# Moving the transposes of the forget gates behind the latent keys, and the scan's row of ones to GpSimd

## The chip, the cores and the metric

The kernel runs on one core of one Trainium2 chip. The core has TensorE (matrix products and transposes, into eight PSUM banks), VectorE, ScalarE, GpSimd, a queue for loads (SP), and DMA engines. The metric is the device time of one execution in microseconds, lower is better; it is given as the median of several runs.

## What is computed

The program is a decoder trunk of two layers over 512 positions of width 1024, in float32. The change lies in the first layer's mixer, of which this is the part that matters:

```python
h = x @ w_in
q_a, c_kv, q_idx, k_idx, w_idx, q_b, k_b, v_b, f_in = _split(h, EVEN_WIDTHS)
q_idx = q_idx.reshape(bsz, seq, H_IDX, D_IDX) * (D_IDX ** -0.5)
w_idx = w_idx * (H_IDX ** -0.5)
log_f = jax.nn.log_sigmoid(f_in + b_f)
cum_f = jnp.cumsum(log_f, axis=1)
...
idx = jnp.einsum('bthd,bsd->bths', qi, k_idx)
score = jnp.einsum('bth,bths->bts', wi, jax.nn.relu(idx))
...
_, sel = lax.top_k(score, k_sel)
...
lb = jnp.einsum('bthd,bshd->bhts', qb, k_b)
lb = lb + jnp.swapaxes(fq, 1, 2)[..., None] - cum_f_keys[:, :, None, :]
```

Eight heads attend over keys chosen by an index score (128 of up to 512), eight others over all earlier keys with a bias made of cumulated logarithms of forget gates. After the mixer come a norm, a convolutional feed-forward part, and the second layer.

## The kernel before

**Products.** All weights come as units of 128 x 1024 float32 through one stream on the SP queue (three raw buffers). Each unit is split into a high part (a cast on ScalarE, line 76) and a low part (a subtraction on VectorE, line 77), and each product is made of three, high by high, high by low and low by high (lines 168 to 170, in `mm3`). A projection (`proj`, line 183) is eight blocks of three products into one PSUM bank. `unit()` hands out the next split unit and has the two after it split too; the units for the values and the first pairs go to larger buffers (lines 387 and 388), and the others share three.

**The first stage** (lines 359 to 410). Two units are computed side by side, one of which gives, for all positions, the index keys in rows 0 to 63, the forget gates in rows 64 to 71 and the index weights in rows 96 to 103. That bank is copied to a temporary buffer `cw` (line 370). On the eight rows of the gates follow the bias (378), the steps of a logarithm of a sigmoid (379 to 382), a row of ones (383, VectorE) and a scan over the positions (384, VectorE) that writes the cumulated gates back into `cw`; they are stored to DRAM (386, GpSimd's queue), from where they are later loaded as biases along the keys. Meanwhile TensorE computes the other three index query projections, whose banks are scaled and split by ScalarE (399) and VectorE (400) in turn.

**Around the change.** Then TensorE transposes `cw` (403 to 405), and ScalarE scales two slices of the result: `nfq` (408), the cumulated gates along the queries, read by GpSimd's bias (line 550), and `wi` (410), the index weights, read by VectorE's accumulation of the scores (453, 455). Behind that stand the projection of the latent keys (413, 414), and the relative-position table: two small products with a one-hot table (422, 428), their copies (424, 430), two round trips through DRAM on GpSimd's queue (426 to 435) and a mask (436). Then the scores: for each of three blocks of positions and eight heads two products (448) into a bank of their own, a rectifier on ScalarE (450) and an accumulation on VectorE (453, 455). Behind them stand the value projections (484 to 489), the attention loop (678 on) with the rounds of the selection on VectorE (467, 469, 472) spread over it, and the rest of the program.

**What sets the order.** The text gives dependencies and priorities; a planner (`schedule_with_timeline_sim=True`) lays out each engine's queue from a timeline of its own and may put a later instruction ahead of an earlier one. On the chip each engine runs its queue in order. Temporary buffers come from a pool of eight, banks from a pool of eight. The selection's rounds are tied to a named VectorE instruction ahead of each (line 468).

Of the kernel before, what the change touches and what calls it, by code (L numbers as in the profile page):

```python
# [9 lines left out]
F32 = mybir.dt.float32  # L10
FR = mybir.dt.float32r
AF = mybir.ActivationFunctionType
ALU = mybir.AluOpType
# [5 lines left out]
NCH = 4  # L19
HD = 64  # L20
NH = 8
# [13 lines left out]
def _f(ap):  # L35
    return ap.bitcast(F32)
# [55 lines left out]
def _body(ctx, tc, A):  # L92
    nc = tc.nc
# [10 lines left out]
    def bank():  # L104
        return ps.tile([128, 512], F32, name="bank")

    def temp():
        return tmp.tile([128, 512], F32, name="temp")
# [7 lines left out]
    def unit():  # L116
        i = base[0]
        base[0] += 1
        return ws.get(i)
# [35 lines left out]
    ident = cst.tile([128, 128], F32)  # L155
# [27 lines left out]
    def proj(w, xt):  # L183
        p = bank()
        half(w, xt, p, 0, S)
        return p
# [8 lines left out]
    def proj_t(us, xt, n):  # L195

        p = bank()
        for k in range(8):
            o = (k % 2) * 512
            last_mm[0] = mm3(p, xk(xt, k, n * 128, n * 128 + 128), wk(us[k // 2], o, o + 512), k == 0, k == 7)  # L200
        return p
# [148 lines left out]
    with ExitStack() as m0:  # L350
        M = m0.enter_context
        mc = M(tc.tile_pool(name="mc", bufs=1))
# [10 lines left out]
        for k in range(8):  # L363
            for u in range(FIRST):
                a = 128 if u else 0
                w = w0[u][1:]
                mm3(p0[u][:, a:], wk(w, k * 128, k * 128 + 128), xk(xq, k, a), k == 0, k == 7)
        p = p0[0]
        cw = temp()
# [4 lines left out]
        nc.vector.tensor_copy(misc[64:128, 1], _f(misc[0:64, 1]))  # L374
        z = temp()
        e = temp()
        g = slice(64, 72)
        nc.scalar.activation(z[g], cw[g], AF.Identity, bias=bf[g])
        nc.vector.scalar_tensor_tensor(out=e[g], in0=z[g], scalar=-1.0, in1=z[g], op0=ALU.mult, op1=ALU.max)
        nc.scalar.activation(e[g], e[g], AF.Exp, scale=-1.0)  # L380
        nc.scalar.activation(e[g], e[g], AF.Ln, bias=1.0)
        nc.vector.scalar_tensor_tensor(out=z[g], in0=z[g], scalar=0.0, in1=e[g], op0=ALU.min, op1=ALU.subtract)
        nc.vector.memset(e[g], 1.0)
        nc.vector.tensor_tensor_scan(out=cw[g], data0=e[g], data1=z[g], initial=0.0, op0=ALU.mult, op1=ALU.add)
        fk_d = dr.tile([NH, S], F32, name="fk_d")
        nc.gpsimd.dma_start(fk_d, cw[g])
        for k in range(6, 10):
# [4 lines left out]
        for m in range(4):  # L392
            if m < FIRST - 1:
                p = p0[1 + m]
            else:
                p = bank()
                half(unit(), xq, p, 128, S)
            for s, (a, b) in enumerate(((slice(0, 64), slice(64, 128)), (slice(64, 128), slice(0, 64)))):
                nc.scalar.mul(qi[s][a, m, late_q], p[a, late_q], float(HD ** -0.5))
                nc.vector.scalar_tensor_tensor(out=qi[s][b, m, late_q], in0=p[a, late_q], scalar=float(HD ** -0.5),  # L400
                                               in1=_f(qi[s][a, m, late_q]), op0=ALU.mult, op1=ALU.subtract)

        p = bank()
        for n in range(NCH):
            nc.tensor.transpose(p[:, n * 128:n * 128 + 128], cw[:, n * 128:n * 128 + 128], ident)
        p3 = p.rearrange("p (a b) -> p a b", a=4)
        nfq = mc.tile([128, NCH, NH], F32)
        nc.scalar.mul(nfq, p3[:, :, 64:72], -1.0)
        wi = mc.tile([128, NCH, NH], F32)
        nc.scalar.mul(wi, p3[:, :, 96:104], float(NH ** -0.5))  # L410


        p = proj(unit(), xq)
# [7 lines left out]
        p = bank()  # L421
# [5 lines left out]
        p = bank()  # L427
# [7 lines left out]
                                      ap=[[383, 128], [128 * 384, NH], [1, 256]]))  # L435
        nc.gpsimd.affine_select(out=T5[:, :, 128:], in_=T5[:, :, 128:], pattern=[[0, NH], [-1, 128]],
                                compare_op=ALU.is_ge, fill=BIG, base=0, channel_multiplier=1)


        sel = [None] + [mc.tile([128, 128 * (j + 1)], F32, name=f"sel{j}") for j in (1, 2, 3)]  # L440
# [45 lines left out]
        for n in range(NCH):  # L486
            p = proj_t(us, xq, n)
# [224 lines left out]
    with ExitStack() as m1:  # L712
        M = m1.enter_context
        mc = M(tc.tile_pool(name="mc1", bufs=1))
# [15 lines left out]
        for n in range(NCH):  # L730
            p = proj_t(us, xt, n)
# [12 lines left out]
            for gi in range(8):  # L744
                nc.vector.tensor_scalar(t[:, gi], t[:, gi], mv[:, gi, 0:1], ve[:, gi:gi + 1],
                                        op0=ALU.subtract, op1=ALU.mult)
# [6 lines left out]
        for n in range(NCH):  # L753
            p = proj_t(us, xt, n)
# [3 lines left out]
        for gp in range(4):  # L758
            p = bank()
# [5 lines left out]
            for j in range(2):  # L765
# [3 lines left out]
                    out=uq[:, :, f], in0=p[:, j * 256:j * 256 + 256].rearrange("p (a b) -> p a b", a=4),  # L769
                    scalar=sb[:, gi:gi + 1], in1=uq[:, :, f], op0=ALU.add, op1=ALU.mult)  # L770
        oq = [quad() for _ in range(4)]
        for ft in range(4):
            p = bank()
# [111 lines left out]
```

## Time and profile before

| | us |
|---|---|
| median of three runs | 1191.61 |
| lowest and highest of them | 1191.40, 1192.16 |
| the profiled execution | 1195.23 |
| its span, first to last instruction | 1193.5 |
| TensorE busy in the span | 1165.9 |
| VectorE, ScalarE, GpSimd busy | 720.0, 471.8, 152.1 |
| mean granted clock of TensorE | 0.988 |

The profile is one execution. "Busy" of TensorE is modelled, since products are pipelined: the start of the next product says more than the length of one. A row of a timeline gives the start, the length, the engine (PE is TensorE, DVE VectorE, ACT ScalarE, POOL GpSimd), the line of the kernel, what it writes and reads, and, in brackets, how long the engine was idle before it and what ended that. The granted clock is a share of the full 2.4 GHz; it has the levels 1.00 and 0.50, and a slice with a change in it shows a mean.

### The profile page before, as it was taken

The page shows a single profiled execution, that of the slowest core. Times are in us where ns is not written, and L with a number is a line of the kernel's source. Part 1 is how long each engine was busy: PE and PEld are TensorE (multiplying, and loading weights), DVE is VectorE, ACT ScalarE, POOL GpSimd, SP SyncE. Part 2 cuts the span into 40 slices and gives each one's busy share as a digit, 9 for nine tenths or more (in the row PEclk, how much of TensorE's full clock was granted, in tenths as well). Part 3 has the DMA queues.
Part 4 walks back from the last instruction along what each step waited for, and adds up shares of the span by engine and source line. Part 5 has one row for each costly group of instructions (what it writes and reads, how often), then busy time and mean ns, then how long its engine had stood idle before and what let it go on. Part 6 is the DMA issues. An engine that isn't in the chain of part 4 may idle for free. (4 is left out here: it accounts for less than half of the span.)

```text
span 1193.5 us, 14505 instructions
## 1 busy us (share of the span) xinstructions
PE 1165.9 (98%) x5519; PEld 968.4 (81%) x5519; DVE 720.0 (60%) x1219; ACT 471.8 (40%) x751; POOL 152.1 (13%) x238
## 2 busy tenths in 40 slices
PE   8899999989999999999999999999999999999997
PEld 7687877778988888888888788889888888888885
DVE  6789988847565666563236974456665656552226
ACT  6615667732334443442123343232444444432221
POOL 1033535303000000010001410003000000010003
PEclk9899999989999999999999999999999999999999
DMA  7434201132132323243334223372223232344221
GB/s 236 162 100 146 89 9 46 65 135 101 54 105 90 102 92 102 93 148 117 129 127 151 98 89 114 120 244 88 71 90 105 90 104 89 123 141 142 88 89 70
DMA packets 39973, 129.89 MB, mean 109 GB/s; under 512 B 5128, under 2 KB 5136, under 8 KB 39904
## 3 DMA queue, kind: packets, MB, share of 16 engines
q1 hardware_dynamic: 34848, 113.26, 29.0%
q0 software_dynamic: 5056, 15.71, 4.1%
q8 instruction: 43, 0.70, 0.2%
q14 instruction: 26, 0.21, 0.1%
HBM read 120.54 MB, written 9.99 MB: 109 GB/s over the span
## 5 line engine op out<-in xcount | busy, mean ns | idle before, releaser
L77 DVE TENSOR_TENSOR wlo<-raw,whi 128x1024 fp32r<-128x1024 f32 x159 | 194.9, 1227 | 291.6 <-ACT whi L76 290.8
L168 PE MATMUL bank<-quad,whi 128*128 128x512 f32 (+2 forms) x932 | 354.7, 382 | 2.6 <-ACT whi L133 1.9
L170 PE MATMUL bank<-quad,wlo 128*128 128x512 f32 (+2 forms) x932 | 354.8, 381 | 0.0
L169 PE MATMUL bank<-quad,whi 128*128 128x512 f32 (+2 forms) x932 | 354.3, 380 | 0.0
L76 ACT CAST whi<-raw 128x1024 fp32r<-128x1024 f32 x159 | 167.4, 1054 | 266.6 <-PE bank L170 119.6
L168 PEld LDWEIGHTS bank<-quad,whi 128*128 128x128 f32 x932 | 175.9, 189 | 36.7 <-ACT whi L133 2.2
L170 PEld LDWEIGHTS bank<-quad,wlo 128*128 128x128 f32 x932 | 176.1, 189 | 32.6
L169 PEld LDWEIGHTS bank<-quad,whi 128*128 128x128 f32 x932 | 176.0, 189 | 32.6
L169 PE MATMUL bank<-wlo,quad 128*128 128x512 f32 x388 | 151.9, 392 | 0.0
L170 PE MATMUL bank<-whi,quad 128*128 128x512 f32 x388 | 151.6, 392 | 0.0
L168 PE MATMUL bank<-whi,quad 128*128 128x512 f32 x388 | 150.4, 392 | 0.0
L168 PE MATMUL bank<-quad 128*128 128x512 f32 (+5 forms) x280 | 99.7, 360 | 0.5 <-ACT quad L206 0.5
L169 PE MATMUL bank<-quad 128*128 128x512 f32 (+5 forms) x280 | 98.6, 353 | 0.7 <-DVE quad L77 0.6
L170 PE MATMUL bank<-quad 128*128 128x512 f32 (+5 forms) x280 | 98.6, 353 | 0.0
L169 PEld LDWEIGHTS bank<-wlo,quad 128*128 128x128 f32 x388 | 73.5, 190 | 15.5
L168 PEld LDWEIGHTS bank<-whi,quad 128*128 128x128 f32 x388 | 73.5, 190 | 15.4
L170 PEld LDWEIGHTS bank<-whi,quad 128*128 128x128 f32 x388 | 73.4, 189 | 15.2
L225 POOL DMA_DIRECT2D temp<-x x24 | 13.2, 548 | 568.0 <-ACT quadx L336 424.6
L305 DVE SCALAR_TENSOR_TENSOR temp<-bank,fcw,temp 128x511 f32<-128x511 f32 x88 | 65.4, 743 | 9.1 <-ACT temp L304 9.1
L307 DVE SCALAR_TENSOR_TENSOR temp<-bank,fcw,temp 128x510 f32<-128x510 f32 x88 | 65.8, 748 | 3.0
L304 ACT ACTIVATE temp<-bank,fcw 128x512 f32<-128x512 f32 x88 | 59.9, 681 | 10.8 <-PE bank L170 10.8
L332 ACT ACTIVATE temp<-temp 128x512 f32<-128x512 f32 x44 | 27.8, 633 | 88.5 <-DVE temp L307 88.5
(148 smaller groups left out, 1280.2 us busy)
## 6 DMA issues: line engine op xcount, KB each, us to landing
raw<-in_ws_dram SPq DMA_DIRECT2D x190, 512.0 KB, 3.5
x<-temp SPq DMA_DIRECT2D x24, 256.0 KB, 2.0
temp<-x POOLq DMA_DIRECT2D x24, 256.0 KB, 3.2
temp<-in_xT_dram SPq DMA_DIRECT2D x8, 256.0 KB, 6.5
temp<-fk_d SPq DMA_DIRECT2D x8, 256.0 KB, 4.9
temp<-in_x_dram POOLq DMA_DIRECT2D x8, 256.0 KB, 3.1
quad<-in_ln_g_dram POOLq DMA_DIRECT2D x4, 512.0 KB, 5.3
quad<-in_ln_b_dram POOLq DMA_DIRECT2D x4, 512.0 KB, 6.0
```

The source lines that it names most:

```text
L76: nc.scalar.copy(hi, t)
L77: dve[0] = nc.vector.tensor_tensor(out=lo, in0=t, in1=_f(hi), op=ALU.subtract)
L168: nc.tensor.matmul(out, a[0], b[0], start=first, stop=False)
L169: nc.tensor.matmul(out, a[0], b[1], start=False, stop=False)
L170: return nc.tensor.matmul(out, a[1], b[0], start=False, stop=last)
L225: nc.gpsimd.dma_start(t, src[n * 128:n * 128 + 128, hf * 512:hf * 512 + 512])
L304: nc.scalar.mul(t, p, cw[:, j, 2:3])
L305: nc.vector.scalar_tensor_tensor(out=t[:, 1:], in0=p[:, :S - 1], scalar=cw[:, j, 1:2], in1=t[:, 1:], op0=ALU.mult, op1=ALU.add)
L307: nc.vector.scalar_tensor_tensor(out=t[:, 2:], in0=p[:, :S - 2], scalar=cw[:, j, 0:1], in1=t[:, 2:], op0=ALU.mult, op1=ALU.add)
L332: nc.scalar.activation(tg, tg, AF.Silu)
```

## The change

The memset of the row of ones (line 383) goes from VectorE, where it reused the buffer `e`, to GpSimd, with a temporary buffer of its own; the scan reads that buffer. The four transposes and the two scalings (403 to 410) are written behind the table's mask (436, 437), so behind the projection of the latent keys and the table products and ahead of the scores. What is computed stays the same.

```diff
--- before.py
+++ after.py
@@ -374,14 +374,15 @@
         nc.vector.tensor_copy(misc[64:128, 1], _f(misc[0:64, 1]))
         z = temp()
         e = temp()
+        one = temp()
         g = slice(64, 72)
         nc.scalar.activation(z[g], cw[g], AF.Identity, bias=bf[g])
         nc.vector.scalar_tensor_tensor(out=e[g], in0=z[g], scalar=-1.0, in1=z[g], op0=ALU.mult, op1=ALU.max)
         nc.scalar.activation(e[g], e[g], AF.Exp, scale=-1.0)
         nc.scalar.activation(e[g], e[g], AF.Ln, bias=1.0)
         nc.vector.scalar_tensor_tensor(out=z[g], in0=z[g], scalar=0.0, in1=e[g], op0=ALU.min, op1=ALU.subtract)
-        nc.vector.memset(e[g], 1.0)
-        nc.vector.tensor_tensor_scan(out=cw[g], data0=e[g], data1=z[g], initial=0.0, op0=ALU.mult, op1=ALU.add)
+        nc.gpsimd.memset(one[g], 1.0)
+        nc.vector.tensor_tensor_scan(out=cw[g], data0=one[g], data1=z[g], initial=0.0, op0=ALU.mult, op1=ALU.add)
         fk_d = dr.tile([NH, S], F32, name="fk_d")
         nc.gpsimd.dma_start(fk_d, cw[g])
         for k in range(6, 10):
@@ -399,15 +400,6 @@
                 nc.scalar.mul(qi[s][a, m, late_q], p[a, late_q], float(HD ** -0.5))
                 nc.vector.scalar_tensor_tensor(out=qi[s][b, m, late_q], in0=p[a, late_q], scalar=float(HD ** -0.5),
                                                in1=_f(qi[s][a, m, late_q]), op0=ALU.mult, op1=ALU.subtract)
-
-        p = bank()
-        for n in range(NCH):
-            nc.tensor.transpose(p[:, n * 128:n * 128 + 128], cw[:, n * 128:n * 128 + 128], ident)
-        p3 = p.rearrange("p (a b) -> p a b", a=4)
-        nfq = mc.tile([128, NCH, NH], F32)
-        nc.scalar.mul(nfq, p3[:, :, 64:72], -1.0)
-        wi = mc.tile([128, NCH, NH], F32)
-        nc.scalar.mul(wi, p3[:, :, 96:104], float(NH ** -0.5))
 
 
         p = proj(unit(), xq)
@@ -435,6 +427,15 @@
                                       ap=[[383, 128], [128 * 384, NH], [1, 256]]))
         nc.gpsimd.affine_select(out=T5[:, :, 128:], in_=T5[:, :, 128:], pattern=[[0, NH], [-1, 128]],
                                 compare_op=ALU.is_ge, fill=BIG, base=0, channel_multiplier=1)
+
+        p = bank()
+        for n in range(NCH):
+            nc.tensor.transpose(p[:, n * 128:n * 128 + 128], cw[:, n * 128:n * 128 + 128], ident)
+        p3 = p.rearrange("p (a b) -> p a b", a=4)
+        nfq = mc.tile([128, NCH, NH], F32)
+        nc.scalar.mul(nfq, p3[:, :, 64:72], -1.0)
+        wi = mc.tile([128, NCH, NH], F32)
+        nc.scalar.mul(wi, p3[:, :, 96:104], float(NH ** -0.5))
 
 
         sel = [None] + [mc.tile([128, 128 * (j + 1)], F32, name=f"sel{j}") for j in (1, 2, 3)]
```

## Rows read from the trace of the kernel before

**Rows 1.** Profile page, part 1, by engine: busy us (share), xinstructions.

```profile
PE 1165.9 (98%) x5519; PEld 968.4 (81%) x5519; DVE 720.0 (60%) x1219; ACT 471.8 (40%) x751; POOL 152.1 (13%) x238
```

**Rows 2.** Who waited for whom, TensorE, whole span: us in total, times, longest us.

```profile
PE bank L405 <- DVE temp L384: 5.9, 1, 5.9
```

**Rows 3.** Timeline of TensorE, 37 to 56 us: start, length, what, [idle before].

```profile
37.83 1.08 PE L405 MATMUL bank<-ident,temp 128*128 128x128 f32 x4 [5.88 <-DVE temp L384]
...
38.56 0.78 PE L168 MATMUL bank<-quad,whi 128*128 128x512 f32 x1
...
46.10 0.81 PE L422 MATMUL bank<-temp,rb 32*8 32x384 f32 x2
...
47.15 8.62 PE L448 MATMUL bank<-quad 128*128 128x256 f32 x48
```

**Rows 4.** Busy time in half microseconds, all engines; PEclk is the granted clock.

```profile
core 0: us, PE busy (x) PEld busy (x) DVE busy (x) ACT busy (x) POOL busy (x), PEclk, DMA share, GB/s
...
35.50:36.00 0.50, 0.00 (x0) 0.00 (x0) 0.47 (x2) 0.24 (x1) 0.00 (x0) 0.80 0.88 319
...
42.50:43.00 0.50, 0.50 (x3) 0.40 (x2) 0.00 (x0) 0.00 (x0) 0.00 (x0) 0.87 1.12 188
```

**Rows 5.** Timeline of ScalarE: the copy of the second chunk of value products.

```profile
66.69 0.59 ACT L206 CAST quad<-bank 128x512 fp32r<-128x512 f32 x1 [4.85 <-PE bank L170]
```

**Rows 6.** Timeline of VectorE, 34 to 48 us.

```profile
34.10 0.48 DVE L383 MEMSET temp<- 8x512 f32 x1 [0.16 <-DVE quad L77]
34.62 1.23 DVE L77 TENSOR_TENSOR quad<-raw,quad 128x1024 fp32r<-128x1024 f32 x1
...
36.47 1.22 DVE L384 TENSOR_TENSOR_SCAN temp<-temp 8x512 f32<-8x512 f32 x1
37.71 0.55 DVE L400 SCALAR_TENSOR_TENSOR quad<-bank,quad 64x384 fp32r<-64x384 f32 x1
...
40.69 0.56 DVE L400 SCALAR_TENSOR_TENSOR quad<-bank,quad 64x384 fp32r<-64x384 f32 x1
47.06 1.23 DVE L77 TENSOR_TENSOR wlo<-raw,whi 128x1024 fp32r<-128x1024 f32 x1 [5.81 <-ACT whi L76]
```

**Rows 7.** Timeline of GpSimd, the first 40 us.

```profile
0.79 0.20 POOL L156 MEMSET ident<- 128x128 f32 x1 [0.29 <-POOLq L874]
...
38.25 0.53 POOL L386 DMA_DIRECT2D fk_d<-temp  x1 [26.12 <-DVE temp L384]
```

**Rows 8.** Timeline of ScalarE, 33 to 50 us.

```profile
33.81 0.99 ACT L399 ACTIVATE quad<-bank 64x384 fp32r<-64x384 f32 x2
...
37.35 1.04 ACT L76 CAST whi<-raw 128x1024 fp32r<-128x1024 f32 x1 [1.61 <-DMA raw<-in_ws_dram]
38.42 0.48 ACT L399 ACTIVATE quad<-bank 64x384 fp32r<-64x384 f32 x1
...
39.04 0.19 ACT L410 ACTIVATE wi<-bank 128x32 f32<-128x32 f32 x1
45.98 1.04 ACT L76 CAST whi<-raw 128x1024 fp32r<-128x1024 f32 x1 [6.75 <-PE bank L169]
...
47.41 0.47 ACT L424 ACTIVATE temp<-bank 8x384 f32<-8x384 f32 x1
...
47.85 2.20 ACT L450 ACTIVATE temp<-bank 128x256 f32<-128x256 f32 x8
```

**Rows 9.** Timeline of TensorE behind a later pause.

```profile
224.92 0.44 PE L168 MATMUL bank<-pt,quad 128*64 128x512 f32 x1 [1.41 <-ACT pt L206]
```

**Rows 10.** Busy time in half microseconds behind that pause, columns as in rows 4.

```profile
227.00:227.50 0.50, 0.50 (x3) 0.07 (x1) 0.50 (x3) 0.00 (x0) 0.20 (x1) 0.50 0.00 0
...
230.00:230.50 0.50, 0.50 (x5) 0.50 (x4) 0.43 (x2) 0.45 (x2) 0.00 (x0) 0.64 0.00 0
```

**Rows 11.** Busy time in two longer stretches, columns as in rows 4.

```profile
62.48:100.00 37.52, 37.52 (x169) 30.93 (x168) 32.45 (x83) 7.72 (x11) 12.29 (x29) 1.00 0.34 100
100.00:190.00 90.00, 90.00 (x480) 70.90 (x479) 82.39 (x224) 57.81 (x149) 39.27 (x80) 1.00 0.22 70
```

**Rows 12.** Timeline of VectorE, the first wait for a bias with the selection.

```profile
190.28 0.69 DVE L604 CUSTOM_DVE_ANT_0 d<-bank,d 128x512 f32<-128x512 f32 x1 [1.58 <-POOL d L567]
```

## The prediction

> **What bounds the kernel now.** The first part of the page is read first: TensorE is busy for 98% of the span and no other engine for more than 60% [rows 1]. So the time is TensorE's own work, its idle stretches and what it does at the lower of its two clocks. The second view is who waited for whom, for TensorE, longest first [rows 2]: the longest wait of the whole span is 5.9 us, once, of line 405 (the transposes of the gates) for line 384 (the scan). The third is TensorE's order of time around it [rows 3]. It has nothing from 31.95 (37.83 less the 5.88 idle) to 37.83; then the four transposes, the 24 products of the latent keys from 38.56, the two small table products (lines 422, 428) from 46.10, and the 48 products of the index scores from 47.15 to about 55.7, where the value products begin. The products of the latent keys read weights and inputs that have long been split; nothing but their place behind the transposes keeps them. The fourth view is the granted clock in half microseconds: it falls in the slice from 35.5 and is back in the slice from 42.5 [rows 4], so the work after the wait runs at the half level (granted 0.50, 1.2 GHz) for some 4.7 us. What this costs: 24 products of 512 columns take 5.44 us at the full level (0.59 + 4.85 between the copies of two chunks [rows 5]); here they take 46.10 - 38.56 = 7.54 [rows 3], 2.1 more. TensorE behind this stage is nearly gapless, so an earlier start of the scores reaches the end unless something else is late.
>
> **The ceiling.** From 31.95 TensorE has the latent keys (5.44), the table products (47.15 - 46.10 = 1.05) and the transposes (0.73 at the half level [rows 3], about 0.4 at the full one, an estimate) to do before the scores: 6.9 us, so they could start at 38.8 and not at 47.15. The transposes then come at 38.4, after the scan's end at 37.69 (36.47 + 1.22 [rows 6]), and wait for nothing. Ceiling: 8.3 us.
>
> **The memset.** VectorE loses 0.48 us and the 0.16 idle before it (line 383 [rows 6]). The scan follows 0.64 earlier (end 37.05), or, if it takes the memset's place at 34.10, ends at 35.3. In the new order no one on TensorE waits for either value, so I book nothing. GpSimd gains a memset of 8 x 512: 0.20 us for 128 columns [rows 7], so about 0.5 by column count, an estimate. GpSimd stands idle for 26.12 us before the gates' store at 38.25 [rows 7], from 12.1 on; behind the memset in its queue stand the one-hot load (wanted by line 422, now at 37) and that store, which waits for the scan anyway. The temporary buffer that it takes comes from the pool of eight that the input splits have left by then. The new wait, of the scan for GpSimd, ends over 20 us before the scan is due: nothing. If that cover failed it would be 0.5 us, and the scan would end at 37.5, still before 38.4.
>
> **What the moved step passes.** It issues four transposes on TensorE and two scalings on ScalarE, and no DMA, so nothing of it stands in the queues of SP and GpSimd. On TensorE it passes the latent products and the table products, which then stand in front of it; on ScalarE the copy of the latent keys and the table's two copies. Its readers are line 453 on VectorE, which needs the scaled weights before the first accumulation, and GpSimd's bias of line 550, which stands in GpSimd's queue behind the whole table chain.
>
> **What is late next: ScalarE and the banks.** The scores need a bank per head, and ScalarE has to empty them. Its order before is: second-last copy of the last index query at 33.81 (the later of two), a weight cast at 37.35 that waited 1.61 for its load, the last index-query copy at 38.42 to 38.90, the two small scalings (0.19 each, about 0.3 together), the next weight cast at 45.98, the copy of the latent keys, the table's copy at 47.41, the first rectifier of the scores at 47.85 [rows 8]. I take this order to stay, with the scalings moved behind the table's copy. The cast that stood at 45.98 waited for the latent products to free its buffer; that is now at 37.2, but its load comes later. The load of the cast at 37.35 could start when VectorE freed a raw buffer at 33.94 (34.10 less the 0.16 idle behind that subtraction) and took 3.41; the next starts at 35.85 (34.62 + 1.23 [rows 6]), so it lands at 39.26. From there the old distances hold: the table's bank is empty 1.90 later (47.88 - 45.98), at 41.2; the first rectifier comes 1.87 + 0.3 later, at 41.4.
> TensorE reaches the scores at 38.8 with the banks of the latent keys, of both table products, of the transposes and of the last index query taken: three of eight are left. Three heads at 0.24 (half of the 0.23 for 512 columns, two products each) end at 39.5; then it stalls until about 41.2: 1.7 us.
> The bank of the last index query is held to 41.25: ScalarE and VectorE read it in turn, 33.81, 37.71, 38.42, 40.69 [rows 6, 8]. [...] Were there no such turn, ScalarE's second read would come at 34.8 and the bank be free with VectorE's read near 38.8, the stall would be shorter by one head and the sum 0.2 better; the rows say that the turns are there.
> **The clock.** A pause of this size has a counterpart: at 224.92 TensorE comes back after 1.41 us, and the clock is at the half level from 227.0 at the latest to past 230.0 [rows 9, 10], 3 us or more; the drop behind the long wait lasts from some point in the slice from 35.5 into that from 42.5. After the stall of 1.7 I expect about 3.4 us at half speed, 1.7 lost. Not all of it counts, since ScalarE's pace (8 rectifiers in 2.20, 0.275 a head [rows 8]) is slower than TensorE's 0.24 in the first eight heads and would have held it for about 0.3 to 0.5. I take 0.5 back.
> **The sum.** 8.3 - 1.7 - 1.7 + 0.5 = 5.4 us. Ends: 8.3 without stall; 4.9 with nothing taken back.
> **VectorE** gains about as much: it idles for 5.81 us before 47.06, waiting for the cast that waits for the latent products [rows 6]; that idle time goes, and 0.64 for the memset. Where TensorE gains more than VectorE, the difference falls into VectorE's 5.1 us of idle time from 62.5 to 100 (37.52 less 32.45 [rows 11]). The table's chain of loads (lines 426 to 436) and the gates' loads start from copies and a scan that come earlier too, so they are not late next.
>
> **How it stands to the median.** The profiled execution took 1195.23 us with a span of 1193.5; the median is 1191.61, 3.6 less. A stretch taken out of TensorE's order counts the same in both: 1191.6 - 5.4 = 1186.2.
>
> **Rivals.**
> A, no half-clock stretch, or hardly a stall: if ScalarE takes the latent keys' copy before the weight cast, it empties banks from 39 on, and TensorE pauses for under 0.5 us; or the pause is there and the clock stays. For it: the order of these two was settled before by a difference of one product. Against: the cast's buffer is free one product before the latent bank, as before. Gain 8.3 - 1.7 = 6.6 to 8.3: 1183.3 to 1185.0.
> B, part is given back at the first head with the selection: there VectorE waits 1.58 us for GpSimd's bias at 190.28 [rows 12], because the selection's last round is late, and TensorE pauses behind it. Between 100 and there VectorE idles for only 7.6 us in 90 (90.00 less 82.39 [rows 11]). If its rounds move up by 2 to 3 us less than TensorE, the gain is 2.5 to 4: 1187.6 to 1189.1.
> C, the change does not do what it says: the order on each queue is settled by a planner, and if it puts the transposes ahead of the latent products again, only the memset's time is left: 0.6 to 2.4 us off the gap (37.05 or 35.3 for 37.69), 1189.2 to 1191.0.
> D, slower: the selection's rounds on VectorE are replanned and end later than now. TensorE then waits at the same place for as long as they are late. It decides from the point where they end as late as before against the clock of the span (all of 5.4 given back); to be slower by 0.2% they must end 2.4 us later still, 7.8 us of lost ground. With them 3 us later: 1194.6. For it: VectorE is 92% busy in this stretch [rows 11]. Against: each round is tied to a named step of the products, which move as one.
>
> **How the numbers follow.** Forecast (4.6 to 6.2 gained) 0.45, A 0.29, B 0.12, C 0.08, D 0.06. A measurement of this kernel can tell about 0.2%, 2.4 us, from no change: bounds 1189.2 and 1194.0. Faster: 0.45 + 0.29 + 0.11 of B = 0.85; no change: 0.09 (C and the rest of B); slower 0.06. The range runs from 1183.0 (A to its end) to 1189.4 (B whole, the start of C); it leaves out about 0.06 for D, 0.07 for C and 0.03 below.
>
> **What would show it.** In the profile after: no wait of line 405 for line 384; line 168 of the latent keys at once behind the last index query, near 31.8, at 0.23 a product; line 405 between lines 428 and 448; the first line 448 near 38.8, then a pause that ends with ScalarE's copies near 41.2; a half-clock stretch of 3 to 4 us after it; value products from about 50.3 and not 55.7; every later stage earlier by the same 5 to 6 us. It is wrong if the pause at the scores is longer than 3 us, if line 405 still stands ahead of the latent products, or if the wait at 190 (then about 185) has grown by more than 2 us.

## The result: 0.5 to 0.85% faster, by two gains of which one was forecast

Beside five runs of the kernel before on its chip (median 1191.77 us), the changed kernel took 1185.69 us (1184.57 to 1188.37): ratio 0.9947, interval [0.9926, 0.9967]. On a second chip, beside nine runs of the kernel before (1194.79), it took 1184.62 us (1182.06 to 1186.47): 0.9915 [0.9901, 0.993]. The forecast was 1186.2.

The profiled execution after took 1188.37 us with a span of 1186.7, the longest of its five. Lines are one higher than before from 377 on; the transposes are now line 433, the scores 449, the copies of the table 416 and 422. First who waited for whom, for TensorE, whole span (us in total, times, longest):

```profile
PE bank L168 <- ACT pt L206: 3.5, 4, 1.4
...
PE bank L449 <- ACT far L422: 0.9, 1, 0.9
PE bank L449 <- DVE quad L401: 0.8, 1, 0.8
```

The 5.9 us for the scan [rows 2] are gone. Two waits at the scores are new, and the row of line 168 for line 206 is shorter too, 3.5 for 5.7; that one lies in the attention loop, 200 us later. Its row in the kernel before:

```profile
PE bank L168 <- ACT pt L206: 5.7, 3, 3.4
```

TensorE's timeline of the stage shows the two in place (start, length, what, [idle before]; the first row is the first latent product, the last the first value product):

```profile
32.68 0.39 PE L168 MATMUL bank<-quad,whi 128*128 128x512 f32 x1
...
38.25 0.81 PE L414 MATMUL bank<-temp,rb 32*8 32x384 f32 x2
38.99 0.38 PE L420 MATMUL bank<-rb,temp 32*128 32x8 f32 x2
39.30 0.66 PE L433 MATMUL bank<-ident,temp 128*128 128x128 f32 x4
39.72 0.96 PE L449 MATMUL bank<-quad 128*128 128x256 f32 x6
41.49 0.47 PE L449 MATMUL bank<-quad 128*128 128x256 f32 x2 [0.82 <-DVE quad L401]
42.88 9.24 PE L449 MATMUL bank<-quad 128*128 128x256 f32 x40 [0.92 <-ACT far L422]
51.96 0.39 PE L168 MATMUL bank<-quad 128*128 128x512 f32 x1
```

The latent products follow the index query at once, the transposes wait for nothing, and the scores begin at 39.72 and not at 47.15 [rows 3]; three heads, a pause, one head, a pause. ScalarE's timeline says what the second pause waits for, and VectorE's what the first one waits for and where the scan now stands:

```profile
38.19 1.04 ACT L76 CAST whi<-raw 128x1024 fp32r<-128x1024 f32 x1 [1.57 <-DMA raw<-in_ws_dram]
39.26 0.49 ACT L400 ACTIVATE quad<-bank 64x384 fp32r<-64x384 f32 x1
40.80 1.04 ACT L76 CAST whi<-raw 128x1024 fp32r<-128x1024 f32 x1 [1.05 <-DMA raw<-in_ws_dram]
41.87 0.58 ACT L206 CAST quad<-bank 128x512 fp32r<-128x512 f32 x1
42.35 0.47 ACT L416 ACTIVATE temp<-bank 8x384 f32<-8x384 f32 x1
42.73 0.15 ACT L422 ACTIVATE far<-bank 128x8 f32<-128x8 f32 x1
```

```profile
33.46 1.23 DVE L77 TENSOR_TENSOR quad<-raw,quad 128x1024 fp32r<-128x1024 f32 x1 [0.31 <-ACT quad L76]
34.72 1.22 DVE L385 TENSOR_TENSOR_SCAN temp<-temp 8x512 f32<-8x512 f32 x1
35.97 1.23 DVE L77 TENSOR_TENSOR quad<-raw,quad 128x1024 fp32r<-128x1024 f32 x1
...
38.40 2.36 DVE L77 TENSOR_TENSOR wlo<-raw,whi 128x1024 fp32r<-128x1024 f32 x2
40.79 0.56 DVE L401 SCALAR_TENSOR_TENSOR quad<-bank,quad 64x384 fp32r<-64x384 f32 x1
```

The weight cast at 40.80 waits for its load with the copies of the latent keys and of the table queued behind it. VectorE's read of the index query's bank at 40.79 follows two splits without a gap. Then the granted clock (PEclk, the third from last number) in half microseconds:

```profile
43.50:44.00 0.50, 0.50 (x7) 0.50 (x6) 0.50 (x2) 0.50 (x4) 0.14 (x1) 1.00 0.84 344
44.00:44.50 0.50, 0.50 (x4) 0.50 (x4) 0.38 (x2) 0.50 (x3) 0.00 (x0) 0.69 0.99 246
...
47.00:47.50 0.50, 0.50 (x3) 0.50 (x2) 0.50 (x3) 0.50 (x2) 0.32 (x1) 0.50 0.00 0
47.50:48.00 0.50, 0.50 (x4) 0.50 (x4) 0.50 (x3) 0.50 (x2) 0.50 (x1) 0.90 0.00 0
```

A mean of 0.69 is 0.62 of a slice, 0.31 us, at the half level, and 0.90 is 0.2 of one, 0.1 us. So the clock is at half from 44.2 to 47.6: 3.4 us.

### The profile page after: what moved, and what is told of

The parts are those of the page before. It is cut to its first block, busy times and chain, and to the rows that moved or that the text cites. A ratio compares the mean times of both kernels' runs of the same rounds, so it can differ in the third digit from the quotient of the medians.

```text
span 1186.7 us, 14513 instructions
## 1 busy us (share of the span) xinstructions
PE 1165.1 (98%) x5519; PEld 969.1 (82%) x5519; DVE 720.0 (61%) x1218; ACT 471.6 (40%) x751; POOL 152.7 (13%) x239
## 5 line engine op out<-in xcount | busy, mean ns | idle before, releaser
L168 PEld LDWEIGHTS bank<-quad 128*128 128x128 f32 (+1 forms) x280 | 52.9, 190 | 12.8 <-issue 3.6
```

What stands on the lines that cost most here:

```text
L168: nc.tensor.matmul(out, a[0], b[0], start=first, stop=False)
```

## The experiments

**How the profiles are compared.** Where a kernel stands when the stage begins differs from one execution to the next: the last product of the index query starts at 32.51 in the first profile of the changed kernel and at 30.80 in the second. So two stretches are read from each TensorE timeline: the *stage*, from the start of that product to the start of the first value product, and the *rest*, from there to the start of the last product of the kernel. In brackets beside each stands for how many us the granted clock was at half in it. Times are medians of 3 to 12 executions, ratios against the kernel before on the same chip; for new_loopZ one execution of 4131.85 us is left out. The last column tells which of four orders the planner gave to the attention loop: it replans this loop with almost every edit of the stage, and the kernels were sorted by their lists of instructions on each engine.

| kernel | median us | ratio [interval] | stage (half) | rest (half) | loop |
|---|---|---|---|---|---|
| before | 1191.61 | | 23.99 (6.8) | 1129.45 (13.6) | B |
| before, again | 1194.65 | 0.9998 [0.9987, 1.001] | 24.20 (6.8) | 1126.91 (6.8) | B |
| changed | 1185.69 | 0.9947 [0.9926, 0.9967] | 19.45 (3.4) | 1126.24 (10.2) | A |
| changed, again | 1184.62 | 0.9915 [0.9901, 0.993] | 19.37 (3.4) | 1124.27 (6.8) | A |
| memset_only | 1188.58 | 0.9949 [0.9936, 0.9961] | 19.16 (none) | 1126.46 (10.2) | M |
| memset_again | 1189.07 | 0.9963 [0.995, 0.9976] | 20.87 (3.4) | 1126.89 (10.2) | M |
| move_only | 1185.18 | 0.9916 [0.9901, 0.9931] | 22.27 (6.8) | 1124.50 (3.4) | A |
| old_loopZ | 1187.47 | 0.9932 [0.9918, 0.9945] | 18.44 (none) | 1125.67 (3.4) | Z |
| new_loopZ | 1189.2 | 0.9949 [0.9936, 0.9963] | 21.79 (6.8) | 1128.53 (10.2) | Z |
| fill5_loopZ | 1187.96 | 0.9939 [0.9926, 0.9951] | 18.12 (none) | 1128.89 (10.2) | Z |
| no_scan_dep | 1184.77 | 0.9934 [0.9916, 0.9951] | 17.67 (none) | 1126.06 (10.2) | A |
| cast_behind | 1184.71 | 0.9916 [0.9903, 0.9929] | 17.67 (none) | 1125.98 (10.2) | A |
| own_row_cast_behind | 1185.60 | 0.9922 [0.9909, 0.9936] | 18.29 (none) | 1126.21 (10.2) | A |
| gp_in_e (see below) | 1184.98 | 0.9925 [0.991, 0.994] | 18.05 (none) | 1126.49 (10.2) | A |

### Controls: both kernels a second time

> The kernel before, a second time, as a control of the comparison and of how far one profiled execution stands for another. Both theories: ratio 1.000 within 0.0015; wait for the scan of 5.5 to 6, with a half-clock stretch behind it; value products 23 to 24 us behind the index query. Open is what lies outside this stage: the half-clock stretches in the attention loop took 13.6 us in the first profile (three of them), 6.8 to 10.2 in those of the changed kernel. If that is the order of the loop, it is 13 again; if it is chance of the execution, it is anywhere from 7 to 14, and the gain of the loop is no effect of the change.

> The changed kernel once more, beside the runs below on one chip. By its own stage (value products at 52.0 us) and the stages of the runs so far: 1184 to 1188 us, 5 to 7 us faster than before. Both theories say the same; it is here to be compared with.

The kernel before gives its own time again within 0.0013, with the same wait and the same half-clock stretch in the stage; so the comparison itself adds nothing. The rest of the kernel before came out 2.5 us shorter in the second profile, with 6.8 us less at the half clock: half of 6.8 is 3.4. How many such stretches the loop has is chance of the execution, and a gain read from one pair of profiles behind the stage is good to some 3 us only, unless that time is taken into account.

### One part alone

> The transposes behind the latent keys, the row of ones still a VectorE memset in the old buffer; the attention loop is in the changed kernel's own order. If the move is the whole gain: 1185 to 1187 us, within 0.7 us of the changed kernel. If the memset counts: slower than the changed kernel by 0.6 us, since VectorE's last copy of the index queries and with it the fourth head's bank come 0.6 later.

```
 # the changed kernel, with the row of ones as before
-        nc.gpsimd.memset(one[g], 1.0)
+        nc.vector.memset(e[g], 1.0)
```

> The row of ones by GpSimd in its own buffer, the transposes still ahead of the latent keys. Theory M (the transposes' place is the gain): the scan only takes the memset's place on VectorE, ends 2.4 us earlier at the most, TensorE still waits 3 us or more and the half clock follows; 0.6 to 2.5 us faster than before. Theory R (the row in a buffer of its own is worth most of it, as the run old_loopZ suggests, where the wait shrank from 5.9 to 1.8 us): TensorE waits for 1.5 to 3.5 us, no or a short half-clock stretch, value products before 53 us, and 4 us or more faster than before.

> The row of ones by GpSimd into a buffer of its own and nothing else, a second time, for a second profiled execution. Theory (the shorter wait of 3.3 us is worth more than its 2.6 us, since no half-clock stretch follows it): wait of 2.5 to 3.5, no half-clock stretch between 30 and 52, value products 19 to 19.5 us behind the index query; 1187.5 to 1189.5. Rival (the first profile was a lucky execution): a half-clock stretch of 3.4 us or more behind the wait, value products 20.5 us or more behind the index query, in an execution of about 1189 to 1190.

```
 # the kernel before, transposes at their old place
-        nc.vector.memset(e[g], 1.0)
+        one = temp()
+        nc.gpsimd.memset(one[g], 1.0)
```

The move alone has the whole gain, 0.9916 for 0.9915. The memset alone has 5.6 to 6.2 us (1194.65 less 1189.07, 1194.79 less 1188.58), and the move adds 4.0 to it on the same chip (1188.58 less 1184.62). The parts overlap, since both work on one wait. (The long stages of move_only and new_loopZ have TensorE there earliest, the last product of the index query at 29.31 and 29.22. It pauses for 2.2 and 2.4 us at the scores, for VectorE's read of the index query's bank, and the half-clock stretch is 6.8. That the engines behind this read still wait for the same loads is the likely reason; no run isolates it. So the length of the stage also depends on when TensorE reaches it: move_only's is only 1.7 to 1.9 us shorter than that of the kernel before, but its value products start at 51.59, 3.8 to 4.0 earlier.) TensorE's timeline at the transposes, memset alone, in its two profiles, with the clock of 35.5 to 39.5 behind each:

```profile
35.76 0.66 PE L406 MATMUL bank<-ident,temp 128*128 128x128 f32 x4 [3.28 <-DVE temp L385]
35.50:39.50 4.00, 3.74 (x19) 3.18 (x20) 3.87 (x6) 2.47 (x5) 0.53 (x1) 1.00 0.71 238
```

```profile
34.86 0.67 PE L406 MATMUL bank<-ident,temp 128*128 128x128 f32 x4 [3.38 <-DVE temp L385]
35.50:39.50 4.00, 4.00 (x13) 3.10 (x12) 3.91 (x5) 1.81 (x4) 0.40 (x1) 0.59 0.58 199
```

The wait falls from 5.88 [rows 3] to 3.3, by 2.6. But the stage is 3.3 to 5.0 shorter (24.20 less 20.87, less 19.16), because behind the shorter wait the half-clock stretch is 3.4 us or none, and not 6.8. The two profiles of this one kernel differ by 1.71 in the stage, half of 3.4. So the rival of memset_again came true: the first profile was the luckier one.

### Where the row of ones is written, and the loop's order

> The kernel before with the row of ones in a temporary buffer of its own, still written by VectorE; the transposes stay ahead of the latent keys. With this the planner lays the attention loop (about 100 to 250 us) in another order, called order Z here, while the stage of the wait stays. Theory S (the gain of the change comes from the stage at 32 to 56 us alone): as the kernel before, within 1 us; TensorE waits 5 to 6 us for the scan and runs 4 to 7 us at the half clock behind it. Theory P (part of the gain comes from the planner's new order in the attention loop): differs from before by 1.5 us or more with the wait unchanged, the difference lying behind 190 us.

```
 # the kernel before
-        nc.vector.memset(e[g], 1.0)
+        one = temp()
+        nc.vector.memset(one[g], 1.0)
```

VectorE's timeline shows that a buffer of its own is enough, without another engine:

```profile
23.70 0.48 DVE L384 MEMSET temp<- 8x512 f32 x1
...
29.47 0.68 DVE L383 SCALAR_TENSOR_TENSOR temp<-temp 8x512 f32<-8x512 f32 x1 [0.46 <-ACT temp L382]
30.19 1.14 DVE L401 SCALAR_TENSOR_TENSOR quad<-bank,quad 64x384 fp32r<-64x384 f32 x2
31.36 1.22 DVE L385 TENSOR_TENSOR_SCAN temp<-temp 8x512 f32<-8x512 f32 x1
```

In a buffer of its own the memset runs at 23.70, long before it is wanted, on VectorE too; in the kernel before it had to follow the last reader of the old buffer and stood between two splits, at 34.10 [rows 6]. TensorE then waits 1.82 us and the clock stays. So the run is not what was expected of it: the wait did not stay at 5 to 6 us, and the 7.3 us gained are no measure of the loop alone. The stage is 1.0 us shorter than the changed kernel's, yet the median is 2.3 us above that of move_only on the same chip. The loop has order Z, which is the likely reason; the two profiled executions lie the other way round, 1184.84 and 1186.28.

> The changed kernel with one and a half more warm-up products at the very start (some 0.7 us, ahead of a wait of TensorE for the first weights that should hide most of it), which makes the planner lay the attention loop in the same order Z as in the run beside it. So this run less the other is the stage alone. Theory S: 4.5 to 5.4 us faster than the run beside it, all of it by the value products near 52 us. Theory P: also 4.5 us or so by the value products, but against the kernel before it shows what order Z does, so that new less before is not the 6 us of the changed kernel unless order Z brings what the changed kernel's own order brings. If the stage were worth nothing at the end: no difference between the two.

```
 # the changed kernel, 1.6 more warm-up products at the start
-WARM = 7
+WARM = 8
...
+        nc.tensor.matmul(q[:, :320], misc[:, 0, :128], misc[:, 0, :320], start=True, stop=True)
```

This run was to be 4.5 to 5.4 us faster than old_loopZ; it is 1.7 slower (1189.2 for 1187.47), since old_loopZ lost most of its wait too and has the shorter stage.

With the same 10.2 us at the half clock, the rest is 1128.53 and 1128.89 in order Z, and 1125.98 to 1126.49 in the five profiles in order A: 2.5 us. At 3.4 us it is 1125.67 (old_loopZ) against 1124.50 (move_only), 1.2 only. Order B against order A at 6.8 us is the kernel before, again, against the changed one, again: 1126.91 less 1124.27 is 2.6. With half of the half-clock time taken off every rest (an estimate), order A has 1120.9 to 1121.4 in six profiles and 1122.8 in move_only, and order B 1122.6 and 1123.5. So the loop gained some 1.2 to 2.6 us. That the order brings it is likely and not shown: move_only has the order without the gain, and no run has order B with a short stage.

### What is late next: the banks and the weight cast

> The changed kernel with one order added: ScalarE's weight cast that stood ahead of the copy of the latent keys and waits for its load is put behind the scaling of the index weights. If that cast is what holds the banks (as the prediction says): the copies start at 39.8 instead of 41.9 by the changed kernel's own times, TensorE's second pause at the scores (0.92 us, behind the table's copy) goes and the first (0.82, for VectorE's copy of the last index query) stays; no half clock or a short one; value products 1 to 2.5 us earlier and the end 1 to 2.5 us earlier than the changed kernel. If the half clock comes all the same: 0 to 1 us.

```
 # the changed kernel; unit 12's cast made to follow the scaling of the index weights
-        nc.scalar.copy(hi, t)
+        c = nc.scalar.copy(hi, t)
+        if i in self.behind:
+            self.tc.add_manual_dep(c.ins, self.behind.pop(i).ins.name, AFTER, reason="...")
...
-        wi = ...; nc.scalar.mul(wi, p3[:, :, 96:104], float(NH ** -0.5))
+        wi = ...; ws.behind[12] = nc.scalar.mul(wi, p3[:, :, 96:104], float(NH ** -0.5))
```

> As cast_behind, and the row of ones by VectorE again, but in its own buffer: the planner then lays it early, the scan right behind the last step of the gates, and the last index query's copies ahead of two weight splits. If TensorE's first pause at the scores is for VectorE's copy of the last index query: both pauses go, no half-clock stretch there, value products at 47 to 49 us, and 1 to 2 us faster than cast_behind, 3 to 4 us faster than the changed kernel. If something else sets the pause: as cast_behind.

```
 # cast_behind, and
-        nc.gpsimd.memset(one[g], 1.0)
+        nc.vector.memset(one[g], 1.0)
```

The engine of the memset makes no difference that can be told, 1185.60 for 1184.71. But the run missed what was expected: not both pauses went, the value products start at 50.21, and it is not 1 to 2 us faster. The first pause did go: one split and not two stands ahead of VectorE's last read of the index query's bank, and four heads start. The second stayed, now behind another weight cast that waits for its load ahead of the copies (ScalarE, then TensorE):

```profile
37.97 0.49 ACT L404 ACTIVATE quad<-bank 64x384 fp32r<-64x384 f32 x1 [1.49 <-DVE quad L405]
39.16 1.05 ACT L77 CAST whi<-raw 128x1024 fp32r<-128x1024 f32 x1 [0.71 <-DMA raw<-in_ws_dram]
```

```profile
41.24 4.15 PE L453 MATMUL bank<-quad 128*128 128x256 f32 x22 [0.84 <-ACT far L426]
```

ScalarE's and TensorE's timelines in cast_behind (lines up to four higher):

```profile
38.34 0.59 ACT L210 CAST quad<-bank 128x512 fp32r<-128x512 f32 x1
38.82 0.47 ACT L420 ACTIVATE temp<-bank 8x384 f32<-8x384 f32 x1
39.20 0.15 ACT L426 ACTIVATE far<-bank 128x8 f32<-128x8 f32 x1
...
39.41 1.03 ACT L77 CAST whi<-raw 128x1024 fp32r<-128x1024 f32 x1
```

```profile
38.10 0.96 PE L453 MATMUL bank<-quad 128*128 128x256 f32 x6
39.98 3.87 PE L453 MATMUL bank<-quad 128*128 128x256 f32 x24 [0.92 <-DVE quad L405]
44.29 4.43 PE L453 MATMUL bank<-quad 128*128 128x384 f32 x18 [0.44 <-ACT temp L455]
48.56 0.39 PE L172 MATMUL bank<-quad 128*128 128x512 f32 x1
```

The pause that waited for the table's copy is gone, no half-clock stretch follows, and the stage is 1.7 us shorter than the changed kernel's: that pause is the weight cast waiting for its load ahead of the copies. The time does not follow: 1184.71 for 1184.62. In the profiles the 1.7 go in the rest, 1125.98 for 1124.27, where the half-clock stretch behind the first head with the selection is 6.8 us in the one and 3.4 in the other. Whether that is chance or comes with the earlier start is open; the intervals of the two ratios allow 1.5 us either way. For the second: in all four profiles of order A without a half-clock stretch in the stage, the stretch near 190 us is 6.8 long; in the three with one it is 6.8, 3.4 and none.

> The kernel before, with the row of ones written by GpSimd, but into the old buffer, which the last step of the logarithms reads until about 31.8; transposes at their old place. The planner's order in the attention loop is the one of the changed kernel. Theory (it is the buffer of its own, not the engine, that lets the scan come earlier): the scan stays behind the steps of the logarithms and a handover to GpSimd and back; TensorE's wait for the scan is 4 to 6 us, followed by a half-clock stretch; value products 23 to 24 us behind the index query, as before; and if the loop's order is worth nothing, 1193 to 1196 (before was 1194.8 on the last chip). Rival 1 (taking the memset off VectorE is what counts): the wait is 3.3 us or less as with GpSimd and a buffer of its own, about 1188.5. Rival 2 (the loop's order is worth 3 us by itself): the wait stays at 4 to 6 and value products at 23 to 24, yet the time is 1190 to 1192.

This expectation is of another kernel than the one that ran: by mistake the run had cast_behind with the memset written earlier in the text, in its own buffer. So it is a repeat of cast_behind (stage 18.05, no half-clock stretch, 1184.98), and the question put there, GpSimd into the old buffer, was not tried.

> The changed kernel with five products of 512 columns into the transposes' own bank just ahead of the transposes (their result is overwritten); the attention loop is in order Z too. They take 1.13 us at the full clock, out of a pause of TensorE of 1.74 us at the scores that is there anyway. If that pause is what drops the clock, and the half clock costs 1.2 to 1.7 us: no half-clock stretch near 44 to 48 us, and the value products, and the end, 1.2 to 1.7 us earlier than in the run new_loopZ. If the clock falls all the same: 0 to 0.4 us later than new_loopZ. If the pause is not set by ScalarE's copies but by the products' own place: 1.1 us later.

```
 # the changed kernel, ahead of the transposes
+        for _ in range(5):
+            nc.tensor.matmul(p, misc[:, 0, :128], misc[:, 0], start=True, stop=True)
```

> The kernel before, with the scan writing a buffer of its own, so that the transposes at their old place (ahead of the latent keys' unit) wait for nothing. It leaves the cumulation out of the query side of the forget gates, so its time is that of the order and not of a usable kernel. The planner's order in the attention loop is the one of the changed kernel. Theory (the move pays because it takes the scan out of TensorE's way, and what is late next are ScalarE and the banks): no wait for the scan; latent products about 0.5 us behind the index query; one or two pauses at the scores of 1.5 to 2 us in sum; value products 19 to 20 us behind the last product of the index query, as in the changed kernel (19.4); time within 1.5 us of the changed kernel's 1184.6 on the last chip. Rival (the place of the transposes matters beyond the wait: here they give their bank back before the scores): the pause at the scores is shorter by a head or more, 0.25 us and up, the clock stays, and value products begin about 17.5 us behind the index query; time 1182.5 to 1183.5.

```
 # the kernel before
-        nc.vector.tensor_tensor_scan(out=cw[g], ...)
+        cs = temp()
+        nc.vector.tensor_tensor_scan(out=cs[g], ...)
...
-        nc.gpsimd.dma_start(fk_d, cw[g])
+        nc.gpsimd.dma_start(fk_d, cs[g])
```

Five products without use in the place of idle time leave one pause of 0.73 us and the full clock, and the stage is 1.3 us shorter than the changed kernel's although TensorE has 1.3 us more to do. Against new_loopZ, in the same order Z, the end is 1.2 us earlier (1187.96 for 1189.2), as was expected; against the changed kernel the time is not better. With the transposes at their old place and nothing to wait for, TensorE's timeline has both pauses too, 1.40 us in sum for 1.74, and no half-clock stretch:

```profile
31.45 0.60 PE L406 MATMUL bank<-ident,temp 128*128 128x128 f32 x4
...
38.51 1.21 PE L449 MATMUL bank<-quad 128*128 128x256 f32 x8
40.81 0.50 PE L449 MATMUL bank<-quad 128*128 128x256 f32 x2 [1.09 <-DVE quad L401]
41.62 7.50 PE L449 MATMUL bank<-quad 128*128 128x256 f32 x38 [0.31 <-ACT far L431]
```

So the old place costs nothing in the stage by itself: what cost was the wait. The stage came as the rival had it, 17.67 and at the full clock: the transposes' bank is free again before the scores, and four heads start instead of three. The time came as the first theory had it, 1184.77, the changed kernel's: as with cast_behind, 1.7 us won in the stage are not seen in the median.

## Why the prediction came out

**The ceiling** holds. The scores were to start at 38.8; the index query is 0.9 later in this execution (32.51 against 31.62 in the kernel before), so 39.7; measured 39.72.

**What is late next** was named rightly and sized 0.5 too small. One pause of 1.7 us was forecast, three heads and then idle to 41.2. Measured from start to start, 6 products of 0.12 from 39.72 end at 40.44 and the next starts at 41.49: 1.05; two more end at 41.73 and the next starts at 42.88: 1.15. Sum 2.2. The first pause ends with VectorE's read of the index query's bank (40.79 + 0.56 = 41.35). The forecast had that bank free at 41.25 in the time of before; VectorE's splits are 0.75 later here (a raw buffer is free at 33.46 + 1.23 = 34.69 and not at 33.94), so at 42.0. It came 0.6 earlier than that, which is the memset's 0.64: in move_only, with the memset, the read ends 7.30 us behind that raw buffer, in the kernel before 7.31, here 6.66.

The turns of the two readers are there, but they are not what holds the bank here: ScalarE's read at 39.26 stands right behind a cast that waited 1.57 us for its load, and VectorE's at 40.79 right behind two splits. Where ScalarE's queue is free, in own_row_cast_behind, it does wait 1.49 us for VectorE's read of the same bank. By the Trainium skill (PSUM — Partial Sum Buffer, PSUM bank collisions raise a hardware error) two engines collide in a bank only where they are in the same quadrant of 32 partitions. These two reads are of rows 64 to 127 and of rows 0 to 63, so by that rule the turn would not be needed; no run here tries it without.

The second pause ends with the table's copy, and this is where the sizing failed: the term is the cast's load. It was to land 5.32 us behind the raw buffer ahead of it (33.94 to 39.26), so at 40.0 in this execution; it landed at 40.80, 6.11 behind.

The forecast gave this load the 3.41 us of the one ahead of it, although that one is still under way for the first 1.5 us (35.85 to 37.35). With the memset and the scan at their old places, in move_only, the two are 1.9 us apart and the second takes 4.4 us (VectorE, then ScalarE):

```profile
32.34 1.23 DVE L77 TENSOR_TENSOR quad<-raw,quad 128x1024 fp32r<-128x1024 f32 x1 [0.32 <-ACT quad L76]
...
34.24 1.22 DVE L77 TENSOR_TENSOR quad<-raw,quad 128x1024 fp32r<-128x1024 f32 x1
```

```profile
39.87 1.04 ACT L76 CAST whi<-raw 128x1024 fp32r<-128x1024 f32 x1 [1.20 <-DMA raw<-in_ws_dram]
```

That is 6.30 behind the raw buffer ahead (32.34 + 1.23 = 33.57). In the kernel before, too, the DMA engines are still at work (share of time and GB/s in the last two columns) after 39.26; TensorE held the cast there, so it did not show:

```profile
39.00:39.50 0.50, 0.50 (x2) 0.37 (x2) 0.50 (x2) 0.23 (x2) 0.00 (x0) 0.50 0.49 160
39.50:40.00 0.50, 0.50 (x3) 0.34 (x2) 0.50 (x2) 0.00 (x0) 0.00 (x0) 0.50 0.05 12
```

That the two loads slow each other is the likely reason; no run isolates it.

**The memset** was booked at nothing, and that holds for the time. The scan did come earlier, but by changing places with a split: it stands at 34.72, ahead of the split that stood at 34.62 [rows 6] and is now at 35.97. By 34.62 + 0.75 that split would have come at 35.37, so its raw buffer is free and its load starts 0.6 later. That did not make the load land later: it took 3.60 us (37.20 to 40.80) and not the 4.4 of move_only. GpSimd's side came out: a memset of 0.52 us at 11.03, for an estimate of 0.5, and no one waits for it. (The 0.5 is luck: 0.20 us for 128 columns gives 0.8 for 512 by column count.) In time, the memset on top of the move is worth nothing that these runs can tell (0.9915 for 0.9916), as booked; in the one profile of the move alone TensorE does wait for the scan, 1.27 us.

**The clock** came out: a half-clock stretch of 3.4 us behind the pause, as forecast, in both profiles of the changed kernel. Two pauses of about 1 us and not one of 1.7 stood ahead of it, so the pause that it was likened to was not the same. What it costs is seen where one kernel has it in one profile and not in the other: 1.71.

**The sum.** 5.4 us were forecast for the stage; measured 23.99 - 19.45 = 4.5 and 24.20 - 19.37 = 4.8. The missing 0.6 to 0.9 is the longer pause (0.5) and what was to be taken back at the scores. Value products were to start at 50.3, 51.2 with the later index query: 51.96.

**The rest** was forecast to move as one, and here the prediction is wrong, to its own luck. The loop gained some 1.2 to 2.6 us, most likely by an order that the planner made anew. In the kernel before TensorE waits 3.40 us at 244.80 and, again, 2.46 at 245.09; in the changed kernel no wait of the loop is over 1.42. It is not the order alone: move_only, with the same order, has one of 2.00. TensorE's longest, before again and changed again:

```profile
245.09 0.50 PE L168 MATMUL bank<-pt,quad 128*128 128x512 f32 x1 [2.46 <-ACT pt L206]
```

```profile
230.98 0.45 PE L168 MATMUL bank<-pt,quad 128*64 128x512 f32 x1 [1.42 <-ACT pt L206]
```

4.5 to 4.8 and 1.2 to 2.6 make 5.7 to 7.4; the two chips gave 6.1 and 10.2. The difference is of the size that one execution differs from another. That the median lies 0.5 us from the forecast is in part luck: the stage gave less than was forecast and the loop something that was not.

**The rivals.** A (no stall, no half clock) did not happen, but cast_behind shows its stage, 17.7, and that its condition was the right one, the order of cast and copies. Its time, 1184.71, is no better than the changed kernel's. B (part given back at the first head with the selection) fell: VectorE waits for the bias there as before, moved with everything else:

```profile
186.64 0.69 DVE L605 CUSTOM_DVE_ANT_0 d<-bank,d 128x512 f32<-128x512 f32 x1 [1.58 <-POOL d L568]
```

C (the transposes stay ahead of the latent products) fell, line 433 stands behind 420. Its price was wrong, though: the memset alone was put at 0.6 to 2.4 us and brought 5.6 to 6.2, since the wait was priced and the half-clock stretch behind it and the loop's order were not. D (replanned rounds end later) had the right mechanism with the wrong sign: there was a replanning, and it most likely helped.

## What to carry to other kernels

Price a wait of TensorE together with the half-clock stretch that follows it: here 2.6 us off a wait were worth 3.3 to 5.0 in the stage, and idle time filled with useless products shortened it by 1.3. A shorter stage need not reach the end: four runs with a stage 1.1 to 1.7 us shorter than the changed kernel's, in the same loop order, took the same time as it. A load that starts while another is under way is not to be priced by the one ahead: here 4.4 us and not 3.4. And before a memset is moved to another engine, ask whether it only waits for the buffer it writes. Under a planner a local edit is also a new order far away; compare the orders before a few us are put down to the edit.

## What was not expected of the hardware

Every half-clock stretch ahead of the kernel's last microseconds was 3.4 or 6.8 us long, in 14 profiles. Whether one follows is not set by the length of the wait alone: behind 3.28 us there was none, behind 3.38 in the same kernel there was one; behind 0.82 and 0.92 there was one, behind 0.92 and 0.44 none. The Trainium skill (TensorE: Matmul & The Clock Gate, HAM oscillation — how this bites in real kernels) has the products behind a long wait for a load start at the lower clock. The waits of 5.88 and 6.03 us in the two profiles of the kernel before, for the scan and not for a load, agree: each has 6.8 us at half. For the shorter waits the runs show no rule.
